# Down projection of a decoder layer: seven-product quads in five of eleven K pairs in both halves, and GpSimd transfers that add partial results in SBUF

## The chip, the cores and the metric

The kernel runs on one core of a Trainium2 chip. Its time is the device time of one execution in microseconds (us), all of it: loading, computing and storing the result. Engines work side by side and meet at semaphores: TensorE (PE) multiplies, VectorE (DVE) and ScalarE (ACT) work on elements, GpSimd (POOL) does small things here and issues some transfers, and SyncE (SP) issues most transfers.

## The reference

One layer of a decoder with 256 tokens of width 2048: an attention and state-space mixer, and then a gated feed-forward part with a hidden width of 5632. Only the last lines concern the change:

```python
h = rms_norm(x, ln_ffn_pre[l])
u = causal_depthwise_conv(h @ w_ffn_up[l], ffn_conv_w[l], ffn_conv_b[l])
gate, up = jnp.split(u, [FFN_HIDDEN], axis=-1)
f = (jax.nn.gelu(gate, approximate=True) * up) @ w_ffn_down[l]
x = x + rms_norm(f, ln_ffn_post[l])
```

`f` is 256 x 2048, the sum over 5632 hidden channels, which are 44 K tiles of 128.

## The kernel before

**Precision and weights.** Every float32 product is made of three matmuls. A weight unit of 128 x 1024 (512 KB) is loaded by SP into a `raw` tile; ACT rounds it into `whi` (line 84), and DVE puts the remainder into `wlo` (line 85). A product is hi x hi, hi x lo and lo x hi (lines 315 to 317, or 1108 to 1110). There are 4 `raw` tiles and 7 of `whi` and `wlo` each, so loading and splitting run up to seven units ahead of PE. Each unit that PE finishes is a `tick()`: it fetches the next unit, and runs functions that were put off by `defer(n, fn)` until n ticks later.

**Two halves.** The hidden channels are worked through in two halves of 22 K tiles. In each half the up projection runs first, with the convolution and the gate on DVE and ACT; the gated K tiles stay in SBUF (`gT`, or `gx` for quads). Then the half's down projection adds to `fa`, the 256 x 2048 sum in SBUF (2 token tiles t of 128, 4 column chunks c of 512). `down_pair(half, c)` makes two chunks at once: columns 0 and 1 of a pair are chunks c and c + 1, with c = 0 for the first pair and c = 2 for the second.

**Plain units and quads.** A pair goes through the 11 pairs of K tiles in the order that a string gives. "0" or "1" is a plain unit: one pair of K tiles for column 0 or 1, 2 x 2 x 3 = 12 matmuls of 512 columns, into two PSUM banks `ph` per column (`pss`). "Q" is a quad: one pair of K tiles for both columns, as a product of 2 x 2 blocks with seven block products in place of eight, 21 matmuls. Its four weight operands are called "same", "other", "two" and "more": the first two are loaded, and DVE makes the other two from them (lines 139, 142 and 143); each is split by ACT (line 135) and DVE (line 144). Three of the seven products go straight into the `ph` banks, and four into banks of their own, `p1`, `p6`, `p7` and `q5` (tiles `pa`), which are shared by all quads of a pair. After the pair's last quad `quad_sums` combines these four and adds them to `fa`. After the last unit of a column `fdone` adds its two `ph` banks to `fa` (line 1028).

The first half uses the string `FIVE` (five quads, 6 + 6 plain units), and the second half `FOUR` (four quads, 7 + 7 plain units). The second half's first pair follows its up projection, and its second pair ends the kernel.

**The second half's additions.** A tile `late` holds a row of weights `wpo`, sent to all partitions by a POOL transfer and multiplied by -0.5 on ACT (line 1180), and three scratch blocks `e[0]` to `e[2]` of 128 x 512. `quad_sums` puts p1, p1 + p6 and p1 + p6 + p7 there and adds or subtracts them, eight DVE operations, four of them deferred in the first pair. `fdone` adds the bank to `fa`, takes the sum of squares on ACT (line 233) and multiplies by `wpo` on DVE (line 1034, deferred for chunks 0 and 1). In the last pair the last five units of column 1 are held back and worked through token tile by token tile (`HOLD`), so that the first tile's end runs beside the second's matmuls. The norm's factor then goes over all of `fa`, and the sum is stored.

**What sets the order.** Each engine runs its instructions in one order, fixed when the program is built by a scheduler that starts from the code's order and the deferred ticks. An instruction that waits holds up all behind it on its engine. POOL issues its transfers in order as well.

Of the kernel before, what the change touches and what calls it, by code (L numbers as in the profile page):

```python
# [9 lines left out]
F32 = mybir.dt.float32  # L10
# [4 lines left out]
ALU = mybir.AluOpType  # L15
# [4 lines left out]
P = 128  # L20
D = 2048
# [6 lines left out]
FF = 5632  # L28
NF = FF // P
HALF = NF // 2  # L30
FIVE, FOUR = "0Q0Q0Q01Q0Q011111", "0Q01Q001Q0Q0011111"
ORDERS = (FIVE, FOUR)
QUADS = max(order.count("Q") for order in ORDERS)
PLAIN = HALF - 2 * QUADS
EPS = 1e-6
# [124 lines left out]
def decoder_layer(ctx, tc, x, xT, win, wdt, wout, wup, wdown, relb, vec, cols, mconv, fconv,  # L160
                  consts, out):
    nc = tc.nc
    ctx.enter_context(nc.allow_non_contiguous_dma(reason="overlapping rows of the bias table"))

    pers = ctx.enter_context(tc.tile_pool(name="pers", bufs=1))
# [12 lines left out]
    def psum(name):  # L178
        return msc.tile([P, 512], F32, name=name, tag="m")

    def tok(t):
        return slice(t * P, (t + 1) * P)

    def chunk(c):
        return slice(c * 512, (c + 1) * 512)
# [46 lines left out]
    def square_sum(dst, src):  # L232
        nc.scalar.activation(junk, src, AF.Square, accum_out=dst)
# [39 lines left out]
    def defer(units, fn, *args):  # L273

        pending.append([units, fn, args])
# [11 lines left out]
    def cols_tile(ps, aT):  # L287
        for u in range(2):
            w = ws.take()
            for j in range(8):  # L290
                cols_part(ps, w, aT, u * 8 + j, j)
            tick()
# [11 lines left out]
    def col_psum():  # L304
        return acc.tile([P, 512], F32, name="pa", tag="a")

    def chunk_psums():
        return [acc.tile([P, 512], F32, name="pa", tag="a") for _ in range(NT)]
# [43 lines left out]
    def down_units(half):  # L352

        found, at = [], half * 44
        for what in 2 * ORDERS[half]:
            if what == "Q":
# [52 lines left out]
    with ExitStack() as mctx:  # L409
# [3 lines left out]
        with ExitStack() as actx:  # L413
# [383 lines left out]
            first = [chunk_psums() for _ in range(2)]  # L797
# [23 lines left out]
        ss = [[pers.tile([P, 4], F32, name=f"ss{n}{t}") for t in range(NT)] for n in range(3)]  # L821
# [203 lines left out]
    def fdone(half, c):  # L1025
        def fn(t, ps):
            f = fa[:, t, chunk(c)]
            nc.vector.tensor_tensor(f, ps, f, op=ALU.add)
            if half == 0:
                return  # L1030
            square_sum(ss[2][t][:, c:c + 1], f)

            def scale():
                nc.vector.tensor_tensor(f, f, wpo[:, chunk(c)], op=ALU.mult)

            def weighted_part(q, z):
                return e[t][:, q - 1536:z - 1536] if q >= 1536 else fa[:, t, q:z]

            if c < 3:
                if c == 2:  # L1040
                    scale()
                else:
                    defer(2 + t, scale)
                return
            nc.vector.tensor_tensor(e[t], f, wpo[:, chunk(c)], op=ALU.mult)
            if t == 1:
                still = ident.bitcast(BF16)
                with tc.issue_after(end[0]):
                    tail = [col_psum() for _ in BYPE]
                    for ps, (q, z) in zip(tail, BYPE):  # L1050
                        nc.tensor.matmul(ps[:, :z - q], ident, xt[:, t, q:z], start=True, stop=False)
                    idle = psum("idle")
                    for _ in range(AFTER):
                        nc.tensor.matmul(idle[:, :S], still[:, :P], still, start=True, stop=True)
            r = late_rsqrt(ss[2][t][:, 3:4], fearly[t], lambda: None)
            if t == 1:
                diag = fp.tile([P, UE], F32, name="diag", tag="ts", bufs=2)[:, :P]
                nc.scalar.activation(diag, ident, AF.Copy, scale=r)
                for ps, (q, z) in zip(tail, BYPE):
                    nc.tensor.matmul(ps[:, :z - q], diag, weighted_part(q, z), start=False, stop=True)  # L1060
                    nc.scalar.copy(xt[:, t, q:z], ps[:, :z - q])
                nc.scalar.dma_start(out=out[0, tok(t), BYDVE:], in_=xt[:, t, BYDVE:])
            for q, z in PIECES[t]:
                x1 = xt[:, t, q:z]
                nc.vector.scalar_tensor_tensor(x1, weighted_part(q, z), r, x1, op0=ALU.mult,
                                               op1=ALU.add)
                nc.sync.dma_start(out=out[0, tok(t), q:z], in_=x1)
        return fn

    def gated(i, ug, uu):  # L1070
        cg = conv_ffn(i, ug)
        nc.scalar.activation(cg, cg, AF.Gelu_apprx_tanh)
        cu = conv_ffn(NF + i, uu)
        k = i % HALF - 2 * ORDERS[i // HALF].count("Q")
        if k < 0:
# [28 lines left out]
    def product(ps, j, block, w, h, first, last):  # L1104
# [4 lines left out]
        nc.tensor.matmul(ps, a, w[1][:, s], start=False, stop=False)  # L1109
        end[0] = nc.tensor.matmul(ps, b, w[0][:, s], start=False, stop=last).ins  # L1110

    def quad_sums(half, c, p1, p6, p7, q5):

        f = [[fa[:, t, chunk(c + n)] for t in range(NT)] for n in range(2)]
        tt = nc.vector.tensor_tensor
        if half == 0:
            nc.scalar.copy(f[0][0], p1)
            tt(f[1][0], p6, f[0][0], op=ALU.add)
            tt(f[0][1], p7, f[1][0], op=ALU.add)
            tt(f[1][1], q5, f[0][1], op=ALU.subtract)  # L1120
            tt(f[1][0], q5, f[1][0], op=ALU.subtract)
            return
        nc.scalar.copy(e[0], p1)
        tt(e[1], p6, e[0], op=ALU.add)
        tt(e[2], p7, e[1], op=ALU.add)
        for n in range(2):
            tt(f[1][n], q5, f[1][n], op=ALU.add)

        def first():
            tt(f[0][0], e[0], f[0][0], op=ALU.add)  # L1130
            tt(f[0][1], e[2], f[0][1], op=ALU.add)

        def second():
            for n in range(2):
                tt(f[1][n], f[1][n], e[1 + n], op=ALU.subtract)

        if c == 0:
            defer(1, first)
            defer(3, second)
        else:  # L1140
            first()
            second()

    def down_pair(half, c):

# [4 lines left out]
        pss = [[psum("ph"), psum("ph")] for _ in range(2)]  # L1150
        begun, done, order = set(), {"Q": 0, "0": 0, "1": 0}, ORDERS[half]
        quads = order.count("Q")
# [42 lines left out]
    for half in range(2):  # L1195
        for i in range(half * HALF, (half + 1) * HALF):
            ps = held_up[2 * i:2 * i + 2]
            for _ in range(2 - len(ps)):
                ps.append(col_psum())
                cols_tile(ps[-1], h2)  # L1200
            us = [summed(p) for p in ps]
            if i < 2:
                defer(5 - 2 * i, gated, i, *us)
            else:
                gated(i, *us)
        if half == 1:
            late = pers.tile([P, D + 1536], F32, name="late", tag="h", bufs=1)
            wpo, e = late[:, :D], [late[:, D + 512 * n:D + 512 * (n + 1)] for n in range(3)]
            aux(out=wpo, in_=row_bcast(V_FFNPOST, D))
        for c in (0, 2):  # L1210
            down_pair(half, c)
# [114 lines left out]
```

## Time and profile before

| | |
|---|---|
| Median of 3 runs | 1099.47 us (1099.16 to 1101.64) |
| The profiled execution, its own time | 1100.45 us |
| Span of its instructions | 1098.7 us |
| TensorE clock granted, mean | 0.999 |
| DMA queues: SP's (q1) / POOL's (q0) | 207.64 MB / 8.59 MB |
| Mean rate of all transfers | 198 GB/s |

Lines of the profile give a start in us from the span's begin, a duration, the engine, the line of the kernel, the operation, output <- inputs, and in brackets how long the engine was idle before it and what ended that. Lines of groups give the busy time, the mean in ns, and the idle time before. Lines of transfers give their count, their size and the median time from issue to landing.

### The profile page before, as it was taken

Reading aid. Unit: us, or ns where it says so; the run is one execution under the profiler, and the core shown is the slowest. Engines: PE = TensorE matmul, PEld = TensorE weight load, DVE = VectorE, ACT = ScalarE, POOL = GpSimd, SP = SyncE. Lnnn points to the kernel's source line nnn. Section 1 sums busy time; section 2 is a strip of 40 time slices with the busy share of each in tenths; the row PEclk is TensorE's granted clock in tenths of the full one; section 3 lists DMA queues with packets and bytes.
Section 4 is the critical chain, followed back from the end, with each engine's and each line's share of the span. In section 5 each row is a group of like instructions: output and inputs, shape, how many; then the busy total and the mean of one; then the engine's idle time right before and its main releaser. Section 6 shows DMA issues by size and latency. Waiting matters only on the chain.

```text
span 1098.7 us, 15910 instructions
## 1 busy us (share of the span) xinstructions
PE 1090.8 (99%) x5848; PEld 936.9 (85%) x5848; DVE 882.8 (80%) x1414; ACT 620.0 (56%) x941; POOL 15.5 (1%) x26
## 2 busy tenths in 40 slices
PE   9999999999999999999999999999999999999997
PEld 8888888888888988888888888888888888888886
DVE  6599976766567699888878999868788787888986
ACT  6656544654554486556565564645555656565552
POOL 0001000000000000000000000000000000000000
PEclk9999999999999999999999999999999999999999
DMA  8758644555587276665655475676665656557562
GB/s 295 294 190 270 191 154 152 176 181 165 188 322 251 70 248 216 207 190 191 190 187 183 142 235 179 228 233 189 191 192 192 191 188 189 182 171 233 171 223 83
DMA packets 61358, 217.59 MB, mean 198 GB/s; under 512 B 7200, under 2 KB 8624, under 8 KB 60384
## 3 DMA queue, kind: packets, MB, share of 16 engines
q1 hardware_dynamic: 59328, 207.64, 58.2%
q0 software_dynamic: 1664, 8.59, 2.3%
q8 instruction: 46, 0.75, 0.3%
q10 hardware_dynamic: 288, 0.35, 0.1%
q14 instruction: 32, 0.26, 0.1%
HBM read 214.44 MB, written 2.11 MB: 197 GB/s over the span
## 4 chain that ended last, share of the span: by engine, by line
PE 93%; DVE 3%; DMA 2%; issue 1%; ACT 1%; SPq 0%; POOLq 0%; ACTq 0%; DVEq 0%
PE pa L251 36%; PE pa L252 18%; PE pa L315 5%; PE pa L316 5%; PE pa L317 5%; PE ph L315 3%; PE ph L316 3%; PE ph L317 3%; DMA raw<-in_wdown_dram 1%; PE pab L251 1%; PE pa L1109 1%; PE pa L1108 1%; PE pa L1110 1%; DVE wlo L85 1%; PE ph L1108 1%; PE ph L1109 1%
## 5 line engine op out<-in xcount | busy, mean ns | idle before, releaser
L84 ACT CAST whi<-raw 128x1024 fp32r<-128x1024 f32 (+2 forms) x353 | 364.7, 1038 | 311.9 <-PE pa L251 183.4
L85 DVE TENSOR_TENSOR wlo<-raw,whi 128x1024 fp32r<-128x1024 f32 (+2 forms) x353 | 424.1, 1207 | 140.5 <-ACT whi L84 133.9
L251 PE MATMUL pa<-h,whi 128*128 128x512 f32 x1360 | 471.7, 394 | 0.0
L252 PE MATMUL pa<-h,wlo 128*128 128x256 f32 x1360 | 379.2, 279 | 0.0
L251 PEld LDWEIGHTS pa<-h,whi 128*128 128x128 f32 x1360 | 255.5, 188 | 57.4
L252 PEld LDWEIGHTS pa<-h,wlo 128*128 128x128 f32 x1360 | 255.4, 188 | 0.0
L251 PE MATMUL pa<-hT,whi 128*128 128x512 f32 x384 | 137.4, 399 | 0.0
L252 PE MATMUL pa<-hT,wlo 128*128 128x256 f32 x384 | 107.2, 281 | 0.0
L251 PEld LDWEIGHTS pa<-hT,whi 128*128 128x128 f32 x384 | 72.6, 189 | 15.7 <-issue 0.2
L1019 DVE SCALAR_TENSOR_TENSOR cfc<-cfu,fcv,cfc 128x255 f32<-128x255 f32 (+1 forms) x176 | 83.2, 478 | 2.0 <-ACT cfc L1017 0.6
L315 PE MATMUL ph<-whi,gT 128*128 128x512 f32 x192 | 74.7, 389 | 0.0
L317 PE MATMUL ph<-whi,gT 128*128 128x512 f32 x192 | 74.7, 389 | 0.0
L316 PE MATMUL ph<-wlo,gT 128*128 128x512 f32 x192 | 74.7, 389 | 0.0
L252 PEld LDWEIGHTS pa<-hT,wlo 128*128 128x128 f32 x384 | 72.4, 189 | 0.5 <-issue 0.2
L135 ACT CAST whi<-ts 128x1024 fp32r<-128x1024 f32 x36 | 37.4, 1048 | 38.7 <-DVE ts L143 21.5
L1017 ACT ACTIVATE cfc<-cfu,fcv 128x256 f32<-128x256 f32 x88 | 52.2, 599 | 3.7 <-DVE cfu L1016 3.7
L144 DVE TENSOR_TENSOR wlo<-ts,whi 128x1024 fp32r<-128x1024 f32 x36 | 43.7, 1221 | 10.9 <-ACT whi L135 10.6
L315 PE MATMUL pa<-whi,hT 128*128 128x512 f32 x128 | 51.2, 400 | 0.0
L315 PE MATMUL pa<-whi,mT 128*128 128x512 f32 x128 | 50.3, 393 | 0.0
L317 PE MATMUL pa<-whi,hT 128*128 128x512 f32 x128 | 50.1, 391 | 0.0
L316 PE MATMUL pa<-wlo,mT 128*128 128x512 f32 x128 | 50.0, 390 | 0.0
L316 PE MATMUL pa<-wlo,hT 128*128 128x512 f32 x128 | 49.9, 390 | 0.0
(272 smaller groups left out, 1387.6 us busy)
## 6 DMA issues: line engine op xcount, KB each, us to landing
raw<-in_wup_dram SPq DMA_DIRECT2D x176, 512.0 KB, 3.5
raw<-in_wdown_dram SPq DMA_DIRECT2D x88, 512.0 KB, 3.8
raw<-in_win_dram SPq DMA_DIRECT2D x85, 512.0 KB, 3.5
raw<-in_wout_dram SPq DMA_DIRECT2D x32, 512.0 KB, 4.0
xsq<-in_x_dram SPq DMA_DIRECT2D x2, 1024.0 KB, 9.2
rows<-acd POOLq DMA_DIRECT2D x4, 512.0 KB, 7.7
xt<-in_x_dram POOLq DMA_DIRECT2D x2, 1024.0 KB, 7.2
xr<-in_xT_dram SPq DMA_DIRECT2D x6, 256.0 KB, 6.3
```

What stands on the lines that cost most here:

```text
L84: nc.scalar.copy(hi[:, s], raw[:, s])
L85: return lambda: nc.vector.tensor_tensor(lo[:, s], raw[:, s], f32(hi[:, s]), op=ALU.subtract)
L135: nc.scalar.copy(hi[:, :n], raw[:, :n])
L144: return lambda: nc.vector.tensor_tensor(lo[:, :n], raw[:, :n], f32(hi[:, :n]), op=ALU.subtract)
L251: nc.tensor.matmul(ps, w[0][:, s], both, start=(k == 0), stop=False)
L252: end[0] = nc.tensor.matmul(ps[:, c], w[1][:, s], hi, start=False, stop=(k == KT - 1)).ins
L315: nc.tensor.matmul(ps, a, w[0][:, s], start=(first and j == 0), stop=False)
L316: nc.tensor.matmul(ps, a, w[1][:, s], start=False, stop=False)
L317: end[0] = nc.tensor.matmul(ps, b, w[0][:, s], start=False, stop=(last and j == 1)).ins
L1017: nc.scalar.activation(c, u, AF.Identity, scale=wv[:, 2:3], bias=wv[:, 3:4])
L1019: nc.vector.scalar_tensor_tensor(c[:, sh:], u[:, :S - sh], wv[:, 2 - sh:3 - sh], c[:, sh:], op0=ALU.mult, op1=ALU.add)
L1108: nc.tensor.matmul(ps, a, w[0][:, s], start=first, stop=False)
```

## The change

Both halves now use `FIVE`. In the second half the additions of the partial results change:

- In the first pair `quad_sums` writes p1, the negated p1 + p6, p1 + p6 + p7 (negated and not) and q5 into five scratch blocks, three of them by ACT, and adds them to `fa` by six POOL transfers that accumulate in SBUF (`add`). Two of these go to a tile to which an earlier one of the six goes.
- In the second pair two of the eight sums are such transfers, and six stay on DVE.
- `fdone` of chunks 0 and 1 copies the bank into a scratch block on ACT and adds it to `fa` by a transfer; the sum of squares and the scaling are put off together by six ticks.
- `late` grows from three scratch blocks to nine.

```diff
-FIVE, FOUR = "0Q0Q0Q01Q0Q011111", "0Q01Q001Q0Q0011111"
-ORDERS = (FIVE, FOUR)
+FIVE = "0Q0Q0Q01Q0Q011111"
+ORDERS = (FIVE, FIVE)
...
     def fdone(half, c):
         def fn(t, ps):
             f = fa[:, t, chunk(c)]
+            def scale():
+                nc.vector.tensor_tensor(f, f, wpo[:, chunk(c)], op=ALU.mult)
+
+            def square_and_scale():
+                square_sum(ss[2][t][:, c:c + 1], f)
+                scale()
+
+            if half == 1 and c < 2:
+                part = e[5 + 2 * c + t]
+                nc.scalar.copy(part, ps)
+                add(f, part)
+                defer(6, square_and_scale)
+                return
             nc.vector.tensor_tensor(f, ps, f, op=ALU.add)
...
-            def scale():
-                nc.vector.tensor_tensor(f, f, wpo[:, chunk(c)], op=ALU.mult)
-
...
             if c < 3:
-                if c == 2:
-                    scale()
-                else:
-                    defer(2 + t, scale)
+                scale()
                 return
...
+    def add(dst, src):
+        nc.gpsimd.dma_start(out=dst, in_=src, accum_op=ALU.add)
+
     def quad_sums(half, c, p1, p6, p7, q5):
...
         nc.scalar.copy(e[0], p1)
-        tt(e[1], p6, e[0], op=ALU.add)
-        tt(e[2], p7, e[1], op=ALU.add)
+        nc.vector.scalar_tensor_tensor(e[1], p6, -1.0, e[0], op0=ALU.mult, op1=ALU.subtract)
+        tt(e[2], e[1], p7, op=ALU.subtract)
+        if c == 0:
+            nc.scalar.copy(e[4], q5)
+            nc.scalar.mul(e[3], e[2], -1.0)
+            for dst, src in ((f[0][0], e[0]), (f[1][0], e[1]), (f[1][1], e[2]), (f[0][1], e[3]),
+                             (f[1][0], e[4]), (f[1][1], e[4])):
+                add(dst, src)
+            return
         for n in range(2):
             tt(f[1][n], q5, f[1][n], op=ALU.add)
-
-        def first():
-            tt(f[0][0], e[0], f[0][0], op=ALU.add)
-            tt(f[0][1], e[2], f[0][1], op=ALU.add)
-
-        def second():
-            for n in range(2):
-                tt(f[1][n], f[1][n], e[1 + n], op=ALU.subtract)
-
-        if c == 0:
-            defer(1, first)
-            defer(3, second)
-        else:
-            first()
-            second()
+            add(f[1][n], e[1 + n])
+        tt(f[0][0], e[0], f[0][0], op=ALU.add)
+        tt(f[0][1], f[0][1], e[2], op=ALU.subtract)
...
-            late = pers.tile([P, D + 1536], F32, name="late", tag="h", bufs=1)
-            wpo, e = late[:, :D], [late[:, D + 512 * n:D + 512 * (n + 1)] for n in range(3)]
+            late = pers.tile([P, D + 9 * 512], F32, name="late", tag="h", bufs=1)
+            wpo, e = late[:, :D], [late[:, D + 512 * n:D + 512 * (n + 1)] for n in range(9)]
```

ACT from the second half's first pair into its second, before. L84 and L135 are the casts of weight units, L233 the sums of squares of chunk 0 (first two) and chunk 1 (last two):

```order
L1123 COPY late<-pa 128x512
L84 CAST whi<-raw 128x1024 x5
L135 CAST whi<-raw 128x1024
L233 ACTIVATE junk,ss_3048<-fa 128x512
L135 CAST whi<-raw 128x512
L233 ACTIVATE junk,ss_3049<-fa 128x512
L135 CAST whi<-ts 128x1024 x2
L84 CAST whi<-raw 128x1024 x2
L233 ACTIVATE junk,ss_3048<-fa 128x512
```

The same place now. L1037 is the copy of a `ph` bank (chunk 0 twice, then chunk 1), and L1138 the negated sum:

```order
L1037 COPY late<-ph 128x512
L1138 ACTIVATE late<-late 128x512
L84 CAST whi<-raw 128x1024
L1037 COPY late<-ph 128x512
L135 CAST whi<-raw 128x1024
L135 CAST whi<-raw 128x512
L233 ACTIVATE junk,ss_3048<-fa 128x512
L135 CAST whi<-ts 128x1024
L233 ACTIVATE junk,ss_3049<-fa 128x512
L135 CAST whi<-ts 128x1024
L84 CAST whi<-raw 128x1024
L1037 COPY late<-ph 128x512 x2
```

The squares of chunk 0 still stand among the casts of the second pair's first quad, but wait for transfers now, and the copies that free chunk 1's banks stand behind them.

POOL's transfers now, all twelve, with what each waits for (DMASW is the landing of an earlier transfer of POOL; DVE and Activation made its source). The first six rows are f[0][0], f[1][0], f[1][1], f[0][1], the second add to f[1][0], and chunk 0's bank of the first token tile:

```order
L1120 DMA fa<-late 128x512 [waits DMASW4_49,DVE_49,Activation_49]
L1120 DMA fa<-late 128x512 [waits DVE_49]
L1120 DMA fa<-late 128x512 [waits DMASW6_49,DVE_49]
L1120 DMA fa<-late 128x512 [waits DMASW7_49,Activation_49]
L1120 DMA fa<-late 128x512 [waits DMASW5_49]
L1120 DMA fa<-late 128x512 [waits DMASW4_49]
L1120 DMA fa<-late 128x512 [waits DMASW6_49,DMASW2_49]
L1120 DMA fa<-late 128x512 [waits DMASW7_49,DMASW3_49,Activation_49]
L1120 DMA fa<-late 128x512 [waits DMASW0_49,Activation_49]
L1120 DMA fa<-late 128x512 [waits DMASW2_49,Activation_49]
L1120 DMA fa<-late 128x512 [waits DVE_49] x2
```

Before, POOL had nothing to do between the transfer of `wpo` and the end. Now each second add to a tile is issued only when the first has landed, and all behind it on POOL wait too.

DVE at the end of the first pair, before: L85 and L144 are the lo parts of weight units, L1124 to L1130 the sums of the quads' products:

```order
L85 TENSOR_TENSOR wlo<-raw,whi 128x1024 x3
L1130 TENSOR_TENSOR fa<-late,fa 128x512
L85 TENSOR_TENSOR wlo<-raw,whi 128x1024 x3
L1124 TENSOR_TENSOR late<-pa,late 128x512
L1127 TENSOR_TENSOR fa<-pa,fa 128x512
L1125 TENSOR_TENSOR late<-pa,late 128x512
L1127 TENSOR_TENSOR fa<-pa,fa 128x512
L85 TENSOR_TENSOR wlo<-raw,whi 128x1024
L1131 TENSOR_TENSOR fa<-late,fa 128x512
```

and now, with L1029 the scaling that waits for a transfer and for ACT's square:

```order
L1134 SCALAR_TENSOR_TENSOR late<-pa,late 128x512
L85 TENSOR_TENSOR wlo<-raw,whi 128x1024
L1135 TENSOR_TENSOR late<-late,pa 128x512
L85 TENSOR_TENSOR wlo<-raw,whi 128x1024 x2
L144 TENSOR_TENSOR wlo<-raw,whi 128x1024
L139 TENSOR_TENSOR ts<-raw 128x1024
L144 TENSOR_TENSOR wlo<-raw,whi 128x512
L142 TENSOR_TENSOR ts<-ts,raw 128x512
L1029 TENSOR_TENSOR fa<-fa,late 128x512
L143 TENSOR_TENSOR ts<-ts,raw 128x512
L144 TENSOR_TENSOR wlo<-ts,whi 128x1024
```

Two sums stay, with one L85 between them and two fewer L85 ahead of the first; the scalings stand where they stood among the next quad's work.

## The prediction

> **What bounds the kernel now.** I read the share of each engine first, then the matmul rows of the last two pairs of down projections in order of time, then the waits of ScalarE (ACT) and VectorE (DVE) around them, and last the transfers. The page's first part says that TensorE (PE) never rests:
>
> ```profile
> PE 1090.8 (99%) x5848; PEld 936.9 (85%) x5848; DVE 882.8 (80%) x1414; ACT 620.0 (56%) x941; POOL 15.5 (1%) x26
> ```
>
> A busy row proves little when matmuls overlap, so look at starts. These are the first matmul of the second half's first pair, the first of its second pair, and the one place of either pair where a start comes late, with the DVE row that ends there:
>
> ```profile
> 973.44 0.39 PE L315 MATMUL ph<-whi,gT 128*128 128x512 f32 x1
> ...
> 1030.59 0.39 PE L315 MATMUL ph<-whi,gT 128*128 128x512 f32 x1
> ...
> 1033.76 0.39 PE L1110 MATMUL pa<-whi,gx 128*128 128x512 f32 x1
> 1034.27 0.50 PE L1108 MATMUL ph<-whi,gx 128*128 128x512 f32 x1
> ...
> 1033.53 0.68 DVE L1028 TENSOR_TENSOR fa<-ph,fa 128x512 f32<-128x512 f32 x1
> ```
>
> The first pair holds 14 plain units of 12 matmuls and 4 quads of 21, 252 in all, in 1030.59 - 973.44 = 57.15 us: one starts every 0.2268 us, although each row lasts 0.39. At 1034.27 the step is 0.51 instead of 0.23: PE waits 0.28 us for line 1028 to empty the bank that the new quad writes. So the price of a matmul is 0.2268 us, and the stage is issue-bound. That DVE and ACT nevertheless run close behind is seen in the windows of the four pairs (first half, then second), after the up projection of the second half:
>
> ```profile
> 730.00:973.40 243.40, 243.40 (x1406) 213.74 (x1405) 196.74 (x315) 138.97 (x211) 0.00 (x0) 1.00 0.59 186
> ...
> 616.47:672.93 56.46, 56.46 (x251) 46.75 (x250) 51.76 (x60) 32.99 (x38) 0.00 (x0) 1.00 0.63 205
> 672.93:729.37 56.44, 56.44 (x250) 46.75 (x249) 49.24 (x53) 31.81 (x33) 0.00 (x0) 1.00 0.66 222
> 973.44:1030.59 57.15, 57.15 (x255) 47.31 (x254) 47.91 (x58) 32.40 (x40) 0.58 (x1) 1.00 0.63 209
> 1030.59:1088.12 57.53, 57.41 (x253) 47.23 (x252) 50.36 (x65) 28.42 (x37) 0.56 (x1) 1.00 0.49 157
> ```
>
> Columns are stretch, length, then busy time of PE, weight load, DVE, ACT, GpSimd (POOL), clock, DMA share and GB/s. The first half already has five quads per pair: 56.46 us, which is 249 matmuls (12 x 12 + 5 x 21) at 0.2268.
>
> **The change part by part.** *Matmuls.* Each pair of the second half becomes 249 matmuls, 3 fewer: 6 x 0.2268 = **-1.36 us**. The 0.28 us wait can go as well, since ACT copies that bank now: at best -1.64.
>
> *DVE and ACT work.* Durations of the forms concerned, over the two pairs:
>
> ```profile
> L85 DVE TENSOR_TENSOR wlo<-raw,whi 128x1024 fp32r<-128x1024 f32 x27 | 32.4, 1219 | 4.5 <-ACT whi L84 4.5
> L144 DVE TENSOR_TENSOR wlo<-ts,whi 128x1024 fp32r<-128x1024 f32 x14 | 17.0, 1220 | 6.9 <-ACT whi L135 6.8
> L142 DVE TENSOR_TENSOR ts<-ts,raw 128x512 f32<-128x512 f32 x6 | 4.1, 682 | 0.0
> L84 ACT CAST whi<-raw 128x1024 fp32r<-128x1024 f32 x26 | 26.5, 1050 | 9.4 <-DMA raw<-in_wdown_dram 5.8 <-PE ph L1110 1.9 <-PE pa L251 1.7
> L135 ACT CAST whi<-raw 128x512 fp32r<-128x512 f32 x7 | 4.3, 614 | 2.4 <-DMA raw<-in_wdown_dram 2.4
> L233 ACT ACTIVATE junk<-fa 128x512 f32<-128x512 f32 x7 | 4.4, 632 | 11.7 <-DVE fa L1028 11.7
> L233 ACT ACTIVATION_READ_ACCUMULATOR junk<-fa 128x1 f32 x7 | 1.3, 186 | 0.0
> L1123 ACT COPY late<-pa 128x512 f32<-128x512 f32 x2 | 1.1, 572 | 0.0
> ```
>
> A quad in place of two plain units costs DVE four wide operations and three narrow ones, less two wide: 4 x 1.22 + 3 x 0.68 - 2 x 1.22 = 4.48 us, 9.0 for two. Twelve sums of 0.68 leave DVE (six in the first pair, two in the second, four of line 1028): -8.2. Net +0.8 us, so 99.1 us in both pairs against 98.3, and still below the first half's 101.0, which ran without a gap. ACT gains three wide casts and a narrow one less two wide per quad (1.66 x 2), and six copies of 0.57: +6.7 us on 60.8 of 114.7. The quad operands of two more K tiles fall into the up projection, where DVE has 46 us to spare. All this I cost at nothing; PE covers it, as it does in the first half.
>
> *The twelve adding transfers.* This is the new thing: 256 KB each, SBUF to SBUF, issued by POOL. What waits behind them, by the order above: ACT's second square of the first pair, behind which stand two weight casts and the copies that free the banks of column 1; DVE's scalings, behind which stand the lo parts of the next quad; and, at the end, line 1041. No row has such a transfer. Call L its time from issue to landing and ask how large L may be.
>
> ```profile
> 1011.54 0.39 PE L315 MATMUL ph<-whi,gT 128*128 128x512 f32 x1
> ...
> 1010.98 1.22 DVE L85 TENSOR_TENSOR wlo<-raw,whi 128x1024 fp32r<-128x1024 f32 x1
> 1012.80 1.23 DVE L85 TENSOR_TENSOR wlo<-raw,whi 128x1024 fp32r<-128x1024 f32 x1 [0.61 <-ACT whi L84]
> ...
> 1016.52 0.68 DVE L1124 TENSOR_TENSOR late<-pa,late 128x512 f32<-128x512 f32 x1
> ```
>
> Let T be the end of the first pair's last quad (1011.54 before). Now four L85 stand ahead of the first sum and five ahead of the second, so they run near T+0.7 and T+2.5. Column 0's unit ends at T+2.7; ACT's copy and the negated sum are done near T+5. Its add lands at T+5+L, the next add to that tile is issued 0.6 later and lands at T+5.6+2L. The second square follows (0.82), two casts (2.1), one copy (0.57): the bank is free at T+9.1+2L. PE wants it after 72 matmuls of column work (16.33), a plain unit (2.72) and three more (0.68): T+19.7. Hence **L up to 5.3** costs nothing. Column 1's second add lands at T+9.7+2L+0.6+L; square, scaling and one lo part (2.7) later PE's second quad wants "two" at T+28.6: 3L up to 15.6, **L up to 5.2**; beyond, PE loses about 3(L-5.2).
>
> The end has its own limit:
>
> ```profile
> 1073.97 0.68 DVE L1124 TENSOR_TENSOR late<-pa,late 128x512 f32<-128x512 f32 x1
> ...
> 1082.46 0.68 DVE L1028 TENSOR_TENSOR fa<-ph,fa 128x512 f32<-128x512 f32 x1
> ...
> 1087.45 0.75 DVE L1065 SCALAR_TENSOR_TENSOR xt<-late,lsr,xt 128x512 f32<-128x512 f32 x1
> 1088.32 0.69 DVE L1028 TENSOR_TENSOR fa<-ph,fa 128x512 f32<-128x512 f32 x1
> ...
> 1069.08 0.39 PE L315 MATMUL ph<-whi,gT 128*128 128x512 f32 x1
> ...
> 713.05 0.39 PE L315 MATMUL ph<-whi,gT 128*128 128x512 f32 x1
> ...
> 715.40 0.68 DVE L1118 TENSOR_TENSOR fa<-pa,fa 128x512 f32<-128x512 f32 x1
> ```
>
> DVE works from the first sum at 1073.97 to 1088.20, when PE is done too: no slack. One L85 (1.13) and two sums (1.2) leave this stretch, which makes 14.23 into 11.9; but PE's part after the last quad shrinks from 84 matmuls to 72, 16.3 us. The first sum came 4.9 us after the last quad here (1069.08) and 2.35 in the first half, whose order the pair now has (713.05); I take 3.6, so DVE is ready at 15.5, 0.8 ahead of PE. Line 1041 comes 6.2 us after the first sum (8.49 less 2.33), the add is issued 1.3 after it: **L up to 4.9**, then 0.8 of slack.
>
> How large is L?
>
> ```profile
> raw<-in_wdown_dram SPq DMA_DIRECT2D x88, 512.0 KB, 3.8
> ...
> rows<-acd POOLq DMA_DIRECT2D x4, 512.0 KB, 7.7
> ...
> out_dram<-xt SPq DMA_DIRECT2D x6, 256.0 KB, 2.4
> ...
> wpost<-in_vec_dram POOLq DMA_DIRECT2D x1, 1024.0 KB, 11.9
> ...
> late<-in_vec_dram POOLq DMA_DIRECT2D x1, 1024.0 KB, 8.3
> ...
> fcv<-in_fconv_dram POOLq DMA_DIRECT2D x1, 176.0 KB, 4.4
> ```
>
> Below it is bounded by 2.4 (256 KB, SyncE's queue, nothing beside it), above by 7.7 (512 KB on POOL's queue, four together). The nearest row is fcv; between it and late, 256 KB cost 4.4 + 80 x 3.9/848 = 4.8. I take 4.8, an estimate under all three limits: no stall. If an add moves twice its size, the same line gives 5.9 for 512 KB.
>
> The Trainium skill, "DMA: Bandwidth & Descriptors", section "Anatomy of one DMA", fits such a transfer as 2.0 us plus bytes over 436 GB/s, that is 2.6 us here as an estimate; the sum by it is -1.64 us with no wait anywhere. The trace does not agree for fcv: the fit gives 2.4 us, the row 4.4.
>
> *Sum.* The profiled execution took 1100.45 us, 1.75 more than its span of 1098.7, and lies 0.98 above the median of 1099.47. Its span becomes 1097.1 to 1097.3 and its time 1098.8 to 1099.1. Against the median: 1099.47 - 1.36 = **1098.1**, or 1097.8 if the 0.28 goes too.
>
> **The rivals.** (1) *Slower: ACT stands at a square and holds the weight casts.* It decides from L: with L = 7.7, as in the burst on POOL's queue, PE loses 3 x 2.5 = 7.5 us between the pairs, and the end 7.7 - 4.9 - 0.8 = 2.0; 1097.8 + 9.5 = **1107.3**. Slower by 3.3 us needs stalls of 4.9, which is L above 6.5. For it: the adds meet weight loads that already keep the DMA engines 63% busy. Against it: weight loads of twice the size land in 3.8 amid the same traffic.
>
> (2) *The gain is given back.* L of 5.9 costs 3 x 0.7 + 0.2 = 2.3 us: **1100.1**, no change that can be told.
>
> (3) *ACT opens the pair late.*
>
> ```profile
> 982.53 1.92 ACT L1180 ACTIVATE late<-late 128x2048 f32<-128x2048 f32 x1 [2.78 <-DMA late<-in_vec_dram]
> ```
>
> The first half has no such row. ACT is free at 984.45; the casts and lo parts of the next unit and of the third quad then end with "more" at about 993.3, and PE, now at its third quad by 991.1, wants it at 994.5. This 1.2 us hides all of it; if the row broadcast lands in 11.9 us like wpost instead of 8.3, PE stands 2.4: **1100.2**.
>
> (4) *POOL's issue waits for DVE.*
>
> ```profile
> 297.74 1.23 DVE L85 TENSOR_TENSOR wlo<-raw,whi 128x1024 fp32r<-128x1024 f32 x1 [1.87 <-ACT whi L84]
> ...
> 297.82 1.13 POOL L806 DMA_DIRECT2D xt<-in_x_dram  x2 [88.24 <-ACT whi L84]
> ```
>
> If each issue had to wait for the DVE operation then running, up to 1.22 us, L would act like 6.0: 2.6 us, **1100.4**. But two issues fit into the very 1.23 us of an L85. The Trainium skill, "SBUF — State Buffer", section "Summary: rules for kernel authors", says that descriptor generation for GpSimd's transfers starves while DVE is in a two- or four-fold mode; this would speak against the change, but by these rows the trace does not show it.
>
> **How the numbers follow.** Chances: forecast 0.52 (1097.5 to 1098.8), rival 2 0.18, rival 3 0.08, rival 4 0.04, rival 1 0.16, something outside the list 0.02. A measurement here can tell about 0.3%, 3.3 us: 1096.2 to 1102.8 counts as no change. PE can give 1.64 us at most, so faster gets 0.02, taken from the forecast; slower is rival 1 and the unknown, 0.18; the same is what is left, 0.80. The range goes from 1097.2 to 1104.5 and leaves out the part of rival 1 with L above about 6.9, some 0.13, and the unknown.
>
> **What would show it.** Right: pairs of 249 matmuls in 56.5 us, no step over 0.3 us, POOL's adds landing in under 5 us. Wrong at the adds: ACT's row of line 233 with idle time ended by a DMA, then a PE wait at line 1115 on ACT's copy. Wrong at the end: line 1041 of column 3 idle before it until an add lands. Wrong at the opening: a PE gap at the third quad. The whole fails if L passes 6.5, or if the adds slow the weight loads themselves.

## The result and the profile after

The changed kernel takes **1107.35 us** (median of 6 runs, 1106.74 to 1107.92) against 1099.40 before: a ratio of 1.0069, 95% interval 1.0056 to 1.0082. Slower by 8 us, where 1.4 less was forecast. The profiled execution took 1106.74 us with a span of 1105.0, 6.3 more than the span before.

Shares of the engines hide this (TensorE is still 99% busy). The matmul rows of the second half's two pairs in order of time (start, duration, engine, line) show where it went; the brackets give the idle time ahead of a row and what ended it:

```profile
972.58 0.39 PE L315 MATMUL ph<-whi,gT 128*128 128x512 f32 x1
...
1029.05 0.39 PE L315 MATMUL ph<-whi,gT 128*128 128x512 f32 x1
...
1032.22 0.39 PE L1117 MATMUL pa<-whi,gx 128*128 128x512 f32 x1
1038.64 0.80 PE L1115 MATMUL ph<-whi,gx 128*128 128x512 f32 x1 [6.03 <-ACT late L1037]
1039.23 0.63 PE L1116 MATMUL ph<-wlo,gx 128*128 128x512 f32 x1
1039.66 0.63 PE L1117 MATMUL ph<-whi,gx 128*128 128x512 f32 x1
```

The first pair, 249 matmuls in 1029.05 - 972.58 = 56.47 us, has no late start: 0.68 shorter than before, its share of the forecast. In the second, 15 matmuls in, the next matmul starts 6.42 us after the one ahead of it instead of 0.23, so TensorE loses 6.19 us to ScalarE's copy of a bank (line 1037). Then the steps are 0.43 us instead of 0.227 for some ten matmuls: of the pair's 64.74 us 56.47 are its 249 matmuls, 6.19 the wait, and the 2.1 left are the slow steps. What held ScalarE and, through it, VectorE:

```profile
1023.87 0.62 ACT L135 CAST whi<-raw 128x512 fp32r<-128x512 f32 x1 [1.36 <-DMA raw<-in_wdown_dram]
1032.71 0.63 ACT L233 ACTIVATE junk<-fa 128x512 f32<-128x512 f32 x1 [8.22 <-DMA fa<-late]
...
1033.34 1.03 ACT L135 CAST whi<-ts 128x1024 fp32r<-128x1024 f32 x1
1035.50 0.63 ACT L233 ACTIVATE junk<-fa 128x512 f32<-128x512 f32 x1 [1.13 <-DMA fa<-late]
...
1037.06 1.04 ACT L84 CAST whi<-raw 128x1024 fp32r<-128x1024 f32 x1
1038.01 1.06 ACT L1037 COPY late<-ph 128x512 f32<-128x512 f32 x2
```

```profile
1033.47 0.69 DVE L1029 TENSOR_TENSOR fa<-fa,late 128x512 f32<-128x512 f32 x1 [7.22 <-ACT junk L233]
```

In the kernel before, the same square waited for VectorE's addition, and less long:

```profile
1022.50 0.63 ACT L233 ACTIVATE junk<-fa 128x512 f32<-128x512 f32 x1 [2.80 <-DVE fa L1028]
```

Now ScalarE stands 8.22 us at the first square (line 233) and 1.13 at the second. Behind them stand the casts, and behind these the two copies that free the banks, done by 1038.6: TensorE's restart. The transfers, by the page's list of issues (queue, count, size, median us from issue to landing), then the adds of 960 to 1030 us and of 1070 to 1095 alone:

```profile
raw<-in_wdown_dram SPq DMA_DIRECT2D x88, 512.0 KB, 4.2
...
fa<-late POOLq DMA_DIRECT2D x12, 256.0 KB, 6.8
```

```profile
fa<-late POOLq DMA_DIRECT2D x8, 256.0 KB, 7.4
```

```profile
fa<-late POOLq DMA_DIRECT2D x2, 256.0 KB, 3.5
```

So L, taken as 4.8, is 6.8 in the median (3.3 to 10.0): 7.4 in the burst behind the first pair, amid weight loads, 3.5 at the end with little beside them. The weight loads beside the adds slow down as well. Those issued between 1010 and 1035 us, in the kernel before and in the changed one:

```profile
raw<-in_wdown_dram SPq DMA_DIRECT2D x9, 512.0 KB, 4.3
```

```profile
raw<-in_wdown_dram SPq DMA_DIRECT2D x8, 512.0 KB, 6.6
```

The span adds up: the second half begins 0.86 us earlier than before, the first pair gives 0.68, the second goes from 57.53 to 64.74 us, and the tail behind it takes 0.63 more; -0.86 - 0.68 + 7.21 + 0.63 = +6.3.

### The profile page after: what moved, and what is told of

Its sections match the earlier page's. It is cut to its first block, busy times and chain, and to the rows that moved or that the text cites. A ratio compares the mean times of both kernels' runs of the same rounds, so it can differ in the third digit from the quotient of the medians.

```text
span 1105.0 us, 15932 instructions
## 1 busy us (share of the span) xinstructions
PE 1090.7 (99%) x5842; PEld 936.4 (85%) x5842; DVE 885.9 (80%) x1414; ACT 625.6 (57%) x950; POOL 26.0 (2%) x38
## 4 chain that ended last, share of the span: by engine, by line
PE 87%; DVE 5%; DMA 3%; issue 2%; ACT 2%; SPq 0%; POOL 0%; POOLq 0%; ACTq 0%; DVEq 0%
PE pa L251 36%; PE pa L252 18%; PE pa L315 5%; PE pa L317 5%; PE pa L316 5%; PE ph L317 2%; PE ph L316 2%; PE ph L315 2%; DMA fa<-late 2%; DVE wlo L144 2%; PE pab L251 1%; DMA raw<-in_wdown_dram 1%; DVE wlo L85 1%; PE pa L1117 1%; PE pa L1116 1%
## 5 line engine op out<-in xcount | busy, mean ns | idle before, releaser
L84 ACT CAST whi<-raw 128x1024 fp32r<-128x1024 f32 (+2 forms) x349 | 360.9, 1038 | 309.9 <-PE pa L251 184.9
L85 DVE TENSOR_TENSOR wlo<-raw,whi 128x1024 fp32r<-128x1024 f32 (+2 forms) x349 | 419.6, 1207 | 140.0 <-ACT whi L84 133.1
L135 ACT CAST whi<-ts 128x1024 fp32r<-128x1024 f32 x40 | 41.4, 1047 | 36.3 <-DVE ts L139 16.2
L144 DVE TENSOR_TENSOR wlo<-ts,whi 128x1024 fp32r<-128x1024 f32 x40 | 48.6, 1222 | 6.3 <-ACT whi L135 6.0
L315 PE MATMUL pa<-whi,mT 128*128 128x512 f32 x128 | 50.3, 393 | 0.0
L317 PE MATMUL pa<-whi,mT 128*128 128x512 f32 x128 | 49.9, 390 | 0.0
```

What stands on the lines that cost most here:

```text
L84: nc.scalar.copy(hi[:, s], raw[:, s])
L85: return lambda: nc.vector.tensor_tensor(lo[:, s], raw[:, s], f32(hi[:, s]), op=ALU.subtract)
L135: nc.scalar.copy(hi[:, :n], raw[:, :n])
L144: return lambda: nc.vector.tensor_tensor(lo[:, :n], raw[:, :n], f32(hi[:, :n]), op=ALU.subtract)
L315: nc.tensor.matmul(ps, a, w[0][:, s], start=(first and j == 0), stop=False)
```

## The experiments

Three theories. **Q**: ScalarE works in order, and squares that wait for slow adds hold the casts and copies behind them. **D**: the adds slow the weight loads, and TensorE would wait wherever the squares stand. **V**: five quads are too much for VectorE in this half. Times are medians of 5 to 11 runs (experiment 8 is a single run); each ratio is to the kernel before on the same chip (medians 1099.3 to 1099.6). Where an edit adds a line, the numbers of later lines are one higher.

**1. Squares later.** The squares and scalings are put off by nine ticks instead of six, and each square is placed behind the last cast that the program has given ScalarE by then (`issue_after`). The first edit below is made at line 135 too.

```diff
-        nc.scalar.copy(hi[:, s], raw[:, s])
+        self.cast = nc.scalar.copy(hi[:, s], raw[:, s]).ins
...
-                square_sum(ss[2][t][:, c:c + 1], f)
+                with tc.issue_after(ws.cast):
+                    square_sum(ss[2][t][:, c:c + 1], f)
...
-                defer(6, square_and_scale)
+                defer(9, square_and_scale)
```

> The changed kernel with one edit: in the second half's first pair the squares of columns 0 and 1 (line 233) and the scalings behind them stand later on ScalarE and VectorE, the first of them behind the third quad's casts instead of between them; the adds, the sums and the matmuls stay. Theory Q (ScalarE's order: a square that waits for adds landing in 7 to 8 us holds the casts and the copies that free the banks): the 6.2 us wait of TensorE at line 1115 and the slow clock behind it (2.0 us) go, adds still land in a median of 6 to 7 us, and the time is 1098 to 1099.5. Theory D (the adds slow the weight loads, so that TensorE waits wherever the squares stand): a wait of 3 us or more stays, 1104 or more. Theory V (with five quads in the second half the work of VectorE is too much): no change, about 1107.

Measured 1101.48 us (1099.62 to 1103.74), ratio 1.0022 (1.0013 to 1.0031). The 6.2 us wait and the slow clock are gone, though the adds land no sooner (median 7.6). That carries Q and takes 6 of the 8 us off; but the median is 2 above what Q expected. Theory D is not refuted by it: weight loads issued between 1010 and 1035 us still need 6.8 us in the median, where experiment 2, with the same order and no adds, has 4.2, and VectorE stands at a weight load of the second pair:

```profile
1031.20 1.23 DVE L139 TENSOR_TENSOR ts<-raw 128x1024 f32<-128x1024 f32 x1 [5.08 <-DMA raw<-in_wdown_dram]
```

TensorE does not stand there, as D would have it, but VectorE loses 5 us. A second profile, in experiment 8, takes that up.

**2. Five quads, no transfer.** In the kernel before:

```diff
-ORDERS = (FIVE, FOUR)
+ORDERS = (FIVE, FIVE)
```

> The kernel before with one edit: the second half takes the order with five quads as well; all sums stay on VectorE, so there is no adding transfer at all. Theories Q and D: 249 matmuls a pair, no wait over 1 us, 1098 to 1099.5, a gain of 1.4 to 0 us less what the tail loses by having twelve matmuls less to hide its sums. Theory V: VectorE falls behind TensorE in the second half, waits of several us at the banks, more than 1102.

Measured 1100.85 (1099.38 to 1102.51), ratio 1.0012 (1.0003 to 1.0020): between the theories. With all sums left on VectorE the fifth quad costs about 1.3 us, although it saves six matmuls. In the profile (1099.40 us, one of the fastest of the eleven) TensorE waits for VectorE at a bank and at a lo part:

```profile
1034.22 0.50 PE L1108 MATMUL ph<-whi,gx 128*128 128x512 f32 x1 [1.37 <-DVE fa L1028]
...
1070.42 0.50 PE L1109 MATMUL pa<-wlo,gx 128*128 128x512 f32 x1 [0.30 <-DVE wlo L144]
```

So V holds in part for this kernel; VectorE is busy for 105.95 us of its two pairs here, against 98.75 in the changed kernel, which moves sums away.

**3. Adds, but four quads.** In the changed kernel:

```diff
-ORDERS = (FIVE, FIVE)
+FOUR = "0Q01Q001Q0Q0011111"
+ORDERS = (FIVE, FOUR)
```

> The changed kernel with one edit: the second half goes back to four quads, the adding transfers stay. Theory Q: the squares still stand between the third quad's casts, so a wait of TensorE for a bank stays, somewhat shorter as the column work behind the last quad is longer by twelve matmuls (2.7 us): 2 to 6 us with a slow clock behind it, 1104 to 1109. Theory V: the wait goes with the fifth quad, 1099 to 1100.5.

Measured 1106.11 (1104.81 to 1107.69), ratio 1.0060 (1.0047 to 1.0073). TensorE stands at the same place, and then steps 0.43 us:

```profile
1038.00 0.79 PE L1115 MATMUL ph<-whi,gx 128*128 128x512 f32 x1 [4.24 <-ACT late L1037]
```

With four quads the adds cost 6.6 us, and with five 6.5 (the changed kernel against experiment 2): it is not the fifth quad.

**4. Copies instead of adds.** The kernel then leaves out the additions: each transfer overwrites its destination.

```diff
-        nc.gpsimd.dma_start(out=dst, in_=src, accum_op=ALU.add)
+        nc.gpsimd.dma_start(out=dst, in_=src)
```

> The changed kernel with one edit: the twelve transfers copy instead of adding (the partial results in their destinations are overwritten, so the second half's down projection is left out of the output in part); issues, order and sizes stay. If the addition makes L long (the destination must be read as well, 512 KB moved for 256): the copies land in 3 to 5 us, TensorE's wait is under 2 us, 1099 to 1101. If the traffic of weight loads beside them or the queue makes it long: they land in a median of 6 us or more, the wait is 4 us or more, 1104 to 1107. POOL's issues last 0.86 us with the addition and 0.55 for the transfers of the kernel before; if the addition sets that, they return to 0.55 here.

Measured 1101.49 (1097.66 to 1104.60), ratio 1.0012 (1.0003 to 1.0021). The profiled run was the slowest of the eleven; its transfers over the whole span, and its adding line's issues (start, duration):

```profile
fa<-late POOLq DMA_DIRECT2D x12, 256.0 KB, 4.8
```

```profile
1013.52 0.54 POOL L1120 DMA_DIRECT2D fa<-late  x1 [39.08 <-ACT late L1133]
```

Copies land in 4.8 us in the median and are issued in 0.54; adds need 6.8 and 0.87. By the same two stretches as above a copy takes 5.1 amid the weight loads and 2.3 at the end: the addition costs 1.2 us alone and 2.3 beside the loads. The median of the runs says that this is most of the loss: 1107.35 becomes 1101.49, just above the 1099 to 1101 expected. The expectation on the wait missed in the profiled run: there the copy under the second square, issued at 1027.08 behind a wait for an earlier one, took 6.8, and TensorE still stood 3.90 us. So a median of 4.8 does not make the chain free: its two links lie in the burst.

**5. One add in a row.**

```diff
-        if c == 0:
+        if c < 0:
             nc.scalar.copy(e[4], q5)
```

> The changed kernel with one edit: the branch of quad_sums for the first pair is gone, so column 0 takes its sums as column 2 does (VectorE adds p1's and the negated sums and q5 itself; two adds instead of six), and a tile of column 0 meets one adding transfer instead of two in a row. The squares stay where they were. Theory Q with its price 2L: of the bank's time T+9.1+2L one L goes; ScalarE's copies of column 0 end near T+9, one L of 7 and the four instructions behind it (4.8 us) later the bank is free at T+21 against a need at T+19.7: a wait of 0 to 2 us, no slow clock, 1100 to 1102. If instead any adding transfer beside the weight loads costs TensorE its wait, whatever its chain: 4 us or more stay, 1104 or more.

Measured 1102.02 (1099.69 to 1103.53), ratio 1.0018 (1.0009 to 1.0027): at the upper edge of Q's range. The profiled run (1103.53, the slowest) has the wait that was to go:

```profile
1036.95 0.50 PE L1115 MATMUL ph<-whi,gx 128*128 128x512 f32 x1 [4.37 <-ACT late L1037]
```

Of three adds issued in a row from 1020.72 the last was issued near 1022.4, and the square that waits for it began at 1032.87, some 10 us later (the longest landing is 10.7). One link of the chain went, and the other grew: L in a burst is no constant, which the price 2L had assumed.

**6. Both edits** (1 and 5 together).

> The two edits together: squares and scalings of columns 0 and 1 later, and column 0 with two adds instead of six. If what the kernel with later squares alone still loses (1101.5 against 1098.1 forecast) comes from the adds, their number or the later tail: 1098.5 to 1100. If it comes from five quads beside VectorE's other work, as the kernel without any add suggests (1100.9): 1100.5 to 1102, with waits of TensorE for VectorE's lo parts or sums.

Measured 1099.42 (1098.16 to 1100.65), ratio 0.9999 (0.9991 to 1.0008). The change with its squares out of the way and its adds cut from twelve to eight is as fast as the kernel before, 2 us faster than edit 1 alone and in the range expected if the adds are what edit 1 still loses. VectorE has more sums here, not fewer (busy 102.06 us in the two pairs against 99.09), so the amount of its work is not what cost those 2 us. What keeps it from the forecast, in the windows (length, busy PE, weight load, VectorE, ScalarE, GpSimd, clock, DMA share, GB/s) and in the matmul rows:

```profile
1036.50:1053.00 16.50, 16.43 (x72) 13.01 (x72) 16.50 (x19) 11.35 (x18) 0.00 (x0) 1.00 0.65 217
1053.00:1071.48 18.48, 17.38 (x76) 13.73 (x75) 17.12 (x18) 11.33 (x13) 0.00 (x0) 1.00 0.62 210
```

```profile
1067.94 0.50 PE L1117 MATMUL pa<-wlo,gx 128*128 128x512 f32 x1 [0.49 <-DVE wlo L144]
...
1070.21 0.50 PE L1117 MATMUL pa<-wlo,gx 128*128 128x512 f32 x1 [0.61 <-DVE wlo L144]
```

VectorE is busy without a pause through the middle of the second pair and delivers lo parts late: with the slow step behind each, about 2 us of TensorE. Ahead of this, until 1032.74, it had stood 2.17 us for a weight load.

**7. Idle matmuls in the wait.** Ahead of the matmul that waits:

```diff
             for ps, block, h in items:
+                if last and not done["Q"] and ps is pss[1][0]:
+                    still = ident.bitcast(BF16)
+                    for _ in range(48):
+                        nc.tensor.matmul(q5[:, :S], still[:, :P], still, start=True, stop=True)
                 product(ps, done["Q"], block, w, h, first(ps),
```

> The changed kernel with one edit: 48 idle matmuls (128x256, bf16, 0.12 us each as in the tail, 5.8 us) stand in TensorE's queue just before the matmul that waits 6.2 us, into a bank that is not yet in use. They add nothing to the result and end before the bank that is waited for is free. If the slow clock after the wait (0.43 us a matmul instead of 0.227, 2.0 us in all) comes from TensorE's standing still: the steps behind the wait are 0.23 at once and the time falls by about 2 us, to 1105.3. If it comes from something else in this place (weights that arrive late, the banks): the steps of 0.43 stay, 1107.3.

Measured 1107.63 (1106.68 to 1108.03), ratio 1.0074 (1.0061 to 1.0086). Half of the expectation came true, and that is the telling half:

```profile
1034.79 3.66 PE L1171 MATMUL pa<-cst 128*128 128x256 bf16 x32
1038.98 0.50 PE L1115 MATMUL ph<-whi,gx 128*128 128x512 f32 x1 [0.54 <-ACT late L1037]
```

(The row shows the last 32 of the 48.) Behind the wait the steps are 0.34 and 0.23 at once, so the slow clock came from standing still. Counted from the second half's start, the last quad's last matmul starts 1.15 us sooner than in the changed kernel (103.51 against 104.66). The end does not move: the last scaling matmuls start at 126.08 against 126.19. VectorE's windows suggest why. In the changed kernel, over the stretch in which first VectorE and then TensorE stood, and from there to the last quad; then in this one, the second stretch:

```profile
1026.20:1038.64 12.44, 6.42 (x30) 4.99 (x28) 4.86 (x7) 4.80 (x9) 1.73 (x2) 0.90 0.82 209
1038.64:1077.47 38.83, 38.83 (x163) 32.00 (x163) 35.81 (x38) 24.34 (x30) 1.75 (x2) 0.95 0.64 195
```

```profile
1038.98:1076.90 37.92, 37.32 (x163) 30.36 (x163) 34.80 (x37) 23.29 (x29) 1.75 (x2) 1.00 0.63 195
```

VectorE worked 4.86 of 12.44 us in the first stretch, and 92% of the time afterwards in both. Its first sum that reads the last quad's products (line 1134) starts 110.94 us after the half's start in the one and 110.82 in the other. So the stall looks like one loss seen from two sides: TensorE's wait, and a backlog of VectorE that sets the end. The 2.1 us of slow clock lie inside the second. This is read from the rows, and no run takes the backlog alone away; at the end VectorE itself waits 0.73 and 1.09 us for casts of late weight units.

**8. The first edit again**, one run for a second profile.

> The kernel with later squares once more, for a second profile, since its runs went from 1099.6 to 1103.7 and the profiled one was the shortest. If the other runs lose in waits of TensorE for VectorE's lo parts of the second pair: more and longer of these (they were 0.5 and 0.6 us) and 1101 to 1103. If they lose at the end, behind the tail's adds: a wait for the last scaling matmuls above 1.4 us.

Measured 1102.54. TensorE stands for VectorE's lo parts at places where the first profile has no wait, here two of them:

```profile
1036.82 0.50 PE L1117 MATMUL pa<-wlo,gx 128*128 128x512 f32 x1 [0.75 <-DVE wlo L144]
...
1053.24 0.50 PE L1117 MATMUL pa<-wlo,gx 128*128 128x512 f32 x1 [0.68 <-DVE wlo L144]
```

All late steps of the pair together cost 4.4 us here and 2.4 there; the tail's wait is even shorter (1.22 against 1.41). So what edit 1 leaves is VectorE's lateness. The first of these waits begins at a weight load, for which VectorE stands as in the first profile; the lo part that TensorE wants comes behind it in VectorE's order:

```profile
1034.40 1.23 DVE L139 TENSOR_TENSOR ts<-raw 128x1024 f32<-128x1024 f32 x1 [5.29 <-DMA raw<-in_wdown_dram]
1035.54 1.22 DVE L144 TENSOR_TENSOR wlo<-ts,whi 128x1024 fp32r<-128x1024 f32 x1
```

Both loads took some 7 us. Counted from the pair's start VectorE can use this one 4.84 us in, against 2.72 in the first profile, and the pair is 2.1 us longer (61.02 against 58.91). That fits theory D in part, adds slowing the weight loads, with VectorE too busy to catch up; no run separates the two.

**9. Scalings on GpSimd**, and **10. without them**, both from the kernel with both edits:

```diff
-                scale()
+                nc.gpsimd.tensor_tensor(f, f, wpo[:, chunk(c)], op=ALU.mult)
```

The second drops that line and puts nothing in its place.

> The kernel with both edits, and the four scalings of columns 0 and 1 (line 1029, 0.69 us each) taken from VectorE to GpSimd, in whose queue they stand between the adds of the two pairs. With both edits VectorE was busy 16.50 of 16.50 us at 1036.5 to 1053 and TensorE waited 0.5 and 0.6 us for its lo parts. If VectorE's 2.8 us are what keeps the fifth quad from paying: these waits go and the time is 1097.8 to 1098.7, the forecast of the change. If GpSimd's operations lengthen VectorE's beside them, or ScalarE or the weight loads are short as well: 1099 to 1100.5.

> The kernel with both edits, the four scalings of columns 0 and 1 left out (the output lacks the last layer norm's weights there): the lower bound for the run beside it. If VectorE is what is short: 1097.5 to 1098.5, no wait of TensorE over 0.3 us before the tail. If not: as with both edits, 1099.4.

On GpSimd: 1102.67 (1101.15 to 1104.42), ratio 1.0032 (1.0019 to 1.0044), worse. Two rows of that profile show one cost:

```profile
1039.17 4.40 POOL L1034 TENSOR_TENSOR fa<-fa,late 128x512 f32<-128x512 f32 x2 [6.29 <-ACT junk L233]
```

```profile
1042.48 2.17 DVE L139 TENSOR_TENSOR ts<-raw 128x1024 f32<-128x1024 f32 x1
```

A scaling takes GpSimd 2.2 us instead of VectorE's 0.69, and VectorE's operation beside it 2.17 instead of 1.22. The Trainium skill, "SBUF — State Buffer", section "SBUF: two separate sides", says that the two engines share a pair of ports that one of them holds for its whole instruction; these rows agree. But the second pair is only 0.4 us longer than with both edits. Most of the profile's 4.8 us more is the end: the sum of line 1134 comes 7.9 us after the last quad instead of 1.4, and the last scaling matmuls wait 4.40 us instead of 0.86.

Without the scalings: 1100.42 (1097.87 to 1101.85), ratio 1.0005 (0.9996 to 1.0014). TensorE has no wait in the second pair any more, as V expected, but the time is not shorter. The scheduler put the tail in another order: this sum stands behind the lo parts of the last two weight loads here too, 7.5 us after the last quad, and the last scaling matmuls wait 3.61 us. So VectorE's work is shown to cost TensorE its waits in the pair; what that is worth in time is not.

**11. Adds by VectorE, squares in place**, and **12. the same with squares later** (from experiments 5 and 6):

```diff
-        nc.gpsimd.dma_start(out=dst, in_=src, accum_op=ALU.add)
+        nc.vector.tensor_tensor(dst, dst, src, op=ALU.add)
```

> The changed kernel with column 0 summed as column 2 is, and every remaining add done by VectorE instead of a transfer; ScalarE still copies the banks of columns 0 and 1 out, and the squares stand where the change put them. A square then waits for VectorE (0.69 us an add) and for no transfer. If landing times are what made ScalarE stand at a square: no wait of TensorE for ScalarE's copies, no slow clock, although the squares stand in the same place: 1098.5 to 1101, by how much VectorE's eight more sums (5.5 us) delay its lo parts. If the place of the squares alone did it: 1105 or more.

> The same with squares and scalings later. The kernel without any transfer but with VectorE reading the banks took 1100.9, with waits of 1.4 us for a bank. If ScalarE's copies take that wait away and VectorE keeps up: 1098.5 to 1099.5, better than the kernel before by up to 0.1%. If VectorE is short: 1100 to 1102.

Measured 1100.07 (1098.05 to 1101.34), ratio 1.0001 (0.9992 to 1.0010), and 1101.44 (1099.90 to 1102.95), ratio 1.0016 (1.0007 to 1.0025). The first is a sharp test of Q: its squares stand in front of the casts and copies as in experiment 5, and wait for VectorE instead of a transfer (the adds' traffic is gone with it). ScalarE's first square in it:

```profile
1024.68 0.63 ACT L233 ACTIVATE junk<-fa 128x512 f32<-128x512 f32 x1 [2.10 <-DVE fa L1120]
```

2.10 us instead of experiment 5's 8.12, and no wait of TensorE for a copy. With experiment 1, where the adds land as late and the squares stand later: neither place nor landing time alone makes the 6 us wait. The second brings nothing: later squares help only against transfers. TensorE waits for VectorE's lo parts in both (up to 0.75 and 1.41 us). No version measured here beats the kernel before.

## Why the prediction was wrong

*PE's price and the first pair.* Right: 0.2268 us a matmul, 0.68 us gained there.

*L.* This step failed: "between it and late, 256 KB cost 4.4 + 80 x 3.9/848 = 4.8", under all three limits, hence "no stall". 4.8 is the median of a **copy** (experiment 4). None of the rows it was read from adds. The addition makes 6.8 of it, 7.4 in the burst. The note "if an add moves twice its size" gave 5.9 and was nearer; it became a rival instead of the forecast. The upper bound of 7.7 was too low for single adds (10.0). The burst's load was named ("the adds meet weight loads") and set aside because weight loads land in 3.8. That is the median of all 88 in the kernel before, without adds. Of the weight loads issued between 1010 and 1035 us, beside the adds, it is 6.6 (4.3 before, 4.2 in experiment 2, 5.0 beside the copies of experiment 4). The prediction named "if the adds slow the weight loads themselves" as a sign of failure, and it happened. And the median of lone transfers is not what two links in a burst pay: in the profile of experiment 4 TensorE stood 3.90 us though L's median was 4.8.

*The chain.* Right: second square, casts, copy, "the bank is free at T+9.1+2L". With T = 1012.73, the last quad's end, the bank was free at 1038.6, T+25.8, so two L make 16.7, of which some 1 us is that the negated sum's add was issued near T+6 instead of T+5. The add under the second square began after a wait for an earlier one and was issued at 1029.20, and the square began at 1035.50, so the later L is 6.3; the earlier, with its wait in the queue, is some 10. T+25.8 less the T+19.7 of the need is 6.1; measured 6.19. The limit of 5.3 was a limit on a mean of two adds in a burst, not on L's median.

*Rival 1* is what happened, with place, engine and line as described, and its 1107.3 is the time measured. That is partly luck: of its two prices, 3(L - 5.2) between the pairs and 2.0 at the end, neither is what was paid. TensorE lost 6.2 at column 1's bank and nothing at the second quad, where no wait shows, and the end was late through VectorE's backlog. Its chance of 0.16 rested on limits and bounds read from transfers that do not add.

*The slow clock* was not foreseen. It shows in the rows, but by experiment 7 it costs nothing at the end here.

*DVE and ACT "costed at nothing".* This failed too. The sum was right: VectorE is busy for 98.75 us of both pairs, 99.1 were forecast. But "still below the first half's 101.0" compares sums over both pairs, and the step "PE covers it" does not follow. The first half has no squares and scalings between its pairs; here they and the lo parts meet in the second pair, where VectorE worked 16.50 of 16.50 us in experiment 6. With the stall gone, experiments 6 and 11 end at 1099.42 and 1100.07, still 1.3 and 2.0 us above the forecast: the 1.36 us of the matmuls are not won in any run. The rest of the 9.3, some 7 to 8, is the stall behind the adds and what follows from it. How the 1.3 to 2.0 divide between VectorE's work, the slower weight loads and the order at the end stays open.

*The tail.* The add there landed in 3.5 us, under its limit of 4.9, and line 1041 did not wait: right. But x, the time from the last quad to the sum that reads its products, was taken as 3.6, between two rows, and was 6.05 (1077.47 to 1083.52). It follows the order in which the scheduler puts the sums among the last lo parts: 1.4 in experiment 6, 7.5 in experiment 10.

*Rivals 3 and 4.* The first pair opened without a gap. POOL's issues were longer, but through the addition (0.87 against 0.54), not through waits for VectorE.

## What to carry to other kernels

Price a transfer by a row that does the same operation in the same traffic: the addition turned 4.8 us into 6.8, up to 10 in a burst, and slowed the weight loads beside it from 4.3 to 6.6. Before work goes to an asynchronous transfer, read on every in-order engine what stands behind the first instruction that needs its result; moving that instruction (experiment 1) or replacing the transfer (experiment 11) each took most of the loss away. A saving on the busiest engine counts only if the next one has slack in that very stretch: in the second pair VectorE had none (experiment 6), and in no run did six matmuls less shorten the time.

## What the runs showed of the hardware

- An adding 256 KB transfer within SBUF lands 1.2 us later than a copy with little beside it (3.5 against 2.3) and 2.3 later amid weight loads (7.4 against 5.1); GpSimd issues it in 0.87 us instead of 0.54.
- Weight loads of 512 KB on SyncE's queue, issued between 1010 and 1035 us, land in a median of 5.3 to 6.8 us in the kernels with twelve adds, 4.7 to 4.9 with eight, 5.0 with twelve copies, and 3.9 to 4.3 without any of these.
- In the second pair, after a wait of 3.9 us or more TensorE's next 7 to 13 matmuls step 0.43 us; after waits up to 1.6 us only the next one is longer, by 0.1. The Trainium skill, "TensorE: Matmul & The Clock Gate", Part 1, names a window of some 3.4 us without work after which the clock is halved, and as long a one with work before it returns; the 3.7 to 6.1 us until the step is back fit it roughly, and with idle matmuls in the wait the slow steps did not come.
- An operation of GpSimd on two blocks in SBUF (2.2 us) lengthened VectorE's beside it from 1.22 to 2.17 us.
